# A hybrid attention layer: GpSimd's scaling of attention weights with a second multiplication by 1.0

## The chip, the cores and the metric

One core of a Trainium2 chip runs the kernel. The metric is the device time of one execution in microseconds (us), lower is better; the median over runs is compared. A core has five engines with queues of their own: TensorE (PE), VectorE (DVE), ScalarE (ACT), GpSimd (POOL) and SyncE (SP), which here only starts DMAs.

## What is computed

A decoder layer on a sequence of 256 tokens of width 1024, in float32. The input is normalised and multiplied by one wide matrix; its columns feed three token mixers and their gates. Cut to what matters here:

```python
z = rmsnorm(x, g_in) @ w_in          # queries, keys, values, gates of three mixers
ya = moba_attention(mq, mk, mv)      # 8 heads of 64; with 256 tokens: causal attention
yb = dsa_attention(dq, dk, dv, ...)  # 8 heads of 64; causal, on the 64 keys an indexer selects
yc = cross_attention(xq, mem_k, mem_v)   # 4 heads of 128 into 256 memory tokens
u = sum(sigmoid(g_b) * ((y_b * silu(gate_b)) @ w_up_b) for b in (a, b, c))
out = rmsnorm(x + u @ w_out, g_final)
```

In both self-attentions (names beginning with m and d) a head's weights are `softmax(scores)`: exponentials divided by their sum over a row.

## The kernel before

Every float32 product is made of three fast ones: each operand is split into a high part (a rounded copy, made by ScalarE) and a low part (the remainder, a subtraction on VectorE), and TensorE adds high x high, high x low and low x high. The weights are streamed in about a hundred blocks (`w0`, `w1`, ...): a DMA on SyncE's queue, the copy on ScalarE (L248), the subtraction on VectorE (L249, mostly 128x1024), and then the block's matmuls (L254 to L256, L280).

The program is a list of steps, one a block of weights. Between the matmuls of a step, and before it, the "side work" of the attentions is put by hand: tables of step numbers (`M_PAIRS` and `D_PAIRS` for the two self-attentions) say after which step a function is called. The instructions of TensorE and GpSimd run in exactly that written order; those of VectorE and ScalarE are put in order by the framework's planner, which simulates the program with estimated costs:

```python
ctx.enter_context(tc.manual_schedule(engines={mybir.EngineType.PE, mybir.EngineType.Pool}))
```

Self-attention goes by pairs of heads. `self_scores` has TensorE make a pair's scores (L470), VectorE add the mask and take the maximum (L602), and ScalarE take exponentials into a tile `pr` (L606: mpr, dpr) with their sums in `st` (mst, dst). `PARTS` are the two halves of the queries: 128 queries on 128 keys (128 columns) and 128 queries on 256 keys (256 columns). Half a step later `self_scale` has VectorE take the reciprocals (L614) and GpSimd multiply the weights in place, one instruction a part (L616). `self_transpose` has TensorE transpose the scaled weights (L625: mtp, dtp), ScalarE and VectorE evacuate them in two parts (L626, L627: mph, mpl, dph, dpl), and `self_values` multiplies them by the values (L640: mya, dya) and adds the two parts (L645, L646: myT, dyT).

GpSimd's other work near these: two copies for the indexer (L439, L440) between head 0's scaling and head 1's of the first attention, and `gate_apply` (L719: a product of a normalised gate and a mixer's output), called behind the last heads of the second. VectorE takes that product up in L720. Cross-attention scales its weights on ScalarE (L672).

Of the kernel before, what the change touches and what calls it, by code (L numbers as in the profile page):

```python
# [11 lines left out]
OP = mybir.AluOpType  # L12
# [98 lines left out]
def hybrid_layer_kernel(  # L111
# [14 lines left out]
    nc = tc.nc  # L126
# [247 lines left out]
    for nm in ORDER:  # L374
# [6 lines left out]
        elif nm[0] == "u":  # L381
            b, c = int(nm[1]), int(nm[2])
# [229 lines left out]
    def self_scale(nm, hd):  # L612
        pr, st = prs[nm, hd]
        nc.vector.reciprocal(st[:, 4:6], st[:, 2:4])  # L614
        for t, c in PARTS:
            nc.gpsimd.tensor_scalar_mul(pr[:, c], pr[:, c], st[:, 4 + t : 5 + t])  # L616

    def self_transpose(nm, hd):
        pr, _ = prs.pop((nm, hd))
# [252 lines left out]
    def attend(nm, starts, bias):  # L872
        for b, (s0, s1) in enumerate(starts):
            at(s0, self_scores, nm, b, bias)
            for e in range(2):
                at(s0 + 0.5 + 0.5 * e, self_scale, nm, 2 * b + e)
                at(s1 + e, self_transpose, nm, 2 * b + e)
                at(s1 + 1 + e, self_values, nm, 2 * b + e)
# [188 lines left out]
```

## Time and profile before

| what | us |
|---|---|
| median of 3 runs | 325.01 |
| the three runs | 324.80 to 327.15 |
| the profiled execution, its own time | 326.02 |
| its span, first to last instruction | 324.2 |
| TensorE busy | 314.7 |
| VectorE busy | 252.8 |
| ScalarE busy | 202.8 |
| GpSimd busy | 55.0 |
| L616 on GpSimd, first attention (16 instructions) | 15.9 |
| L616 on GpSimd, second attention (16 instructions) | 15.0 |

Busy times are unions over one engine's instructions in the profiled execution. Matmuls are pipelined and the profile models their ends, so a busy TensorE is not one at its peak. Times on GpSimd are rougher than the others.

### The profile page before, as it was taken

What the parts mean: (1) busy time and instruction counts of PE and PEld (TensorE: products, weight loads), DVE (VectorE), ACT (ScalarE), POOL (GpSimd) and SP (SyncE); (2) the same over time, 40 slices, a digit from 0 to 9 for tenths busy, and PEclk for the clock granted to TensorE, in tenths of its full rate; (3) what the DMA queues carried; (4) which work ended last, traced back from release to release, by engine and by line L of the source; (5) the groups of instructions that cost most, each with busy time, mean ns of one, the idle gap of its engine ahead of it and who ended that gap; (6) DMA issues with size and microseconds to landing.
All of it is one profiled execution on the core that took longest, in us unless ns stands there. A gap on an engine that the chain in (4) does not pass through costs nothing.

```text
span 324.2 us, 6395 instructions
## 1 busy us (share of the span) xinstructions
PE 314.7 (97%) x2442; PEld 299.5 (92%) x2442; DVE 252.8 (78%) x458; ACT 202.8 (63%) x357; POOL 55.0 (17%) x58
## 2 busy tenths in 40 slices
PE   8999999998999999999999999999999999999992
PEld 7799999998999989889999998999999999999882
DVE  3579999998899999987776659998567775677523
ACT  5599766687777636396567596755454546643434
POOL 0000000029305000020400473321000111014011
PEclk9999999999999999999999999999999999999998
DMA  6999887865536346474343433478766566655003
GB/s 203 373 342 312 243 265 215 282 207 147 182 127 169 100 152 232 134 257 142 139 121 130 139 116 120 141 235 284 220 182 195 184 193 198 178 157 189 2 0 129
DMA packets 18367, 59.45 MB, mean 183 GB/s; under 512 B 2208, under 2 KB 2464, under 8 KB 18336
## 3 DMA queue, kind: packets, MB, share of 16 engines
q1 hardware_dynamic: 17760, 57.73, 55.9%
q10 hardware_dynamic: 576, 1.31, 1.1%
q8 instruction: 19, 0.31, 0.4%
q14 instruction: 12, 0.10, 0.1%
HBM read 55.89 MB, written 1.05 MB: 176 GB/s over the span
## 4 chain that ended last, share of the span: by engine, by line
PE 71%; DVE 15%; issue 4%; ACT 4%; DMA 2%; POOL 1%; SPq 1%; DVEq 0%; ACTq 0%; POOLq 0%
DMA w2r<-w_in 2%; PE i_0ps L280 2%; PE i_1ps L280 2%; DVE wk L498 2%; PE mv_0ps L280 1%; PE mv_1ps L280 1%; DVE m L496 1%; PE o_0ps L255 1%; PE o_0ps L254 1%; PE o_0ps L256 1%; POOL dpr L616 1%; PE dya L640 1%; PE lg L480 1%; PE o_1ps L256 1%; PE o_1ps L255 1%
## 5 line engine op out<-in xcount | busy, mean ns | idle before, releaser
L616 POOL TENSOR_SCALAR dpr<-dpr,dst 128x128 f32<-128x128 f32 (+1 forms) x16 | 15.0, 955 | 75.5 <-DVE dst L614 75.5
L616 POOL TENSOR_SCALAR mpr<-mpr,mst 128x128 f32<-128x128 f32 (+1 forms) x16 | 15.9, 1009 | 54.7 <-DVE mst L614 54.7
L745 POOL TENSOR_TENSOR u<-u,gt 128x512 f32<-128x512 f32 x7 | 9.9, 1412 | 77.1 <-DVE gt L742 77.1
L732 ACT ACTIVATE gt<-gt,x_first 128x256 f32<-128x256 f32 x24 | 10.9, 500 | 2.7 <-DVE gt L729 2.7
L606 ACT ACTIVATE dpr<-dms,dst 128x128 f32<-128x128 f32 (+1 forms) x16 | 7.1, 446 | 3.6 <-DVE dst L602 3.6
L786 ACT ACTIVATE junk<-xn 128x512 f32<-128x512 f32 (+1 forms) x5 | 2.7, 543 | 8.6 <-DVE xn L784 8.6
L606 ACT ACTIVATE mpr<-mms,mst 128x128 f32<-128x128 f32 (+1 forms) x16 | 7.1, 444 | 1.2 <-DVE mst L602 1.2
L662 ACT ACTIVATE xpr<-xsc,xst,xs_rstd 128x256 f32<-128x256 f32 x8 | 4.4, 560 | 3.3 <-DVE xst L658 3.3
L750 ACT CAST us<-u 128x512 fp32r<-128x512 f32 x4 | 2.5, 622 | 6.1 <-POOL u L745 4.9
L645 ACT COPY dyT<-dya 64x256 f32<-64x256 f32 x8 | 2.9, 367 | 4.2 <-PE dya L640 4.1
L484 ACT ACTIVATE rl<-lg 128x384 f32<-128x384 f32 x8 | 3.9, 484 | 2.7 <-PE lg L480 1.6
L487 DVE SCALAR_TENSOR_TENSOR acc<-rl,iw,acc 128x128 f32<-128x128 f32 (+1 forms) x14 | 5.3, 425 | 0.1
L790 POOL TENSOR_TENSOR xn<-xn,gf 128x512 f32<-128x512 f32 x2 | 2.6, 1288 | 16.0 <-ACT junk L786 16.0
L480 PE MATMUL lg<-ikT,iqT 128*128 128x128 f32 (+1 forms) x32 | 5.1, 281 | 0.1
L966 PE MATMUL warm<-ones 128*128 128x128 f32 x18 | 4.2, 430 | 1.0 <-DVE eps_t L961 1.0
L602 DVE CUSTOM_DVE_ANT_0 mms<-msc,bias_c 128x128 f32<-128x128 f32 (+1 forms) x16 | 5.0, 350 | 0.0
L966 PEld LDWEIGHTS warm<-ones 128*128 128x128 f32 x18 | 3.9, 331 | 1.0 <-DVE eps_t L961 1.0
L646 DVE TENSOR_TENSOR dyT<-dyT,dya 64x256 f32<-64x256 f32 x8 | 3.3, 417 | 1.9 <-ACT dyT L645 1.7
L627 DVE TENSOR_TENSOR dpl<-dtp,dph 128x384 fp32r<-128x384 f32 x8 | 4.4, 554 | 0.4
L602 DVE CUSTOM_DVE_ANT_0 dms<-dsc,sel 128x128 f32<-128x128 f32 (+1 forms) x16 | 4.7, 351 | 0.0
L626 ACT CAST dph<-dtp 128x384 fp32r<-128x384 f32 x8 | 3.8, 479 | 1.4 <-PE dtp L625 1.3
L784 DVE TENSOR_TENSOR xn<-o_0ps,xn 128x512 f32<-128x512 f32 x2 | 1.4, 692 | 4.2 <-PE o_0ps L256 4.2
(1296 smaller groups left out, 1546.1 us busy)
## 6 DMA issues: line engine op xcount, KB each, us to landing
x_rows<-x SPq DMA_DIRECT2D x2, 512.0 KB, 8.1
eT<-memT SPq DMA_DIRECT2D x4, 256.0 KB, 4.7
xn<-x SPq DMA_DIRECT2D x2, 512.0 KB, 5.7
w0r<-w_in SPq DMA_DIRECT2D x2, 256.0 KB, 3.4
w1r<-w_in SPq DMA_DIRECT2D x2, 256.0 KB, 5.1
xT<-xT SPq DMA_DIRECT2D x2, 256.0 KB, 6.8
w2r<-w_in SPq DMA_DIRECT2D x1, 512.0 KB, 7.3
w3r<-w_in ACTq DMA_DIRECT2D x1, 512.0 KB, 7.7
```

The source lines that it names most:

```text
L255: nc.tensor.matmul(ps, ah, bl, start=False, stop=False)
L256: nc.tensor.matmul(ps, al, bh, start=False, stop=last)
L280: nc.tensor.matmul(accs[nm][t][:, :n], a[p](k, slice(t * P, (t + 1) * P)), w[q][:, half, :], start=k + i == 0, stop=k + i == nk + 1,)
L480: nc.tensor.matmul(lg[:, c : c + n], q[:, q0:q1], idx["k"][:, j, 0:n], start=j == 0, stop=j == 1)
L487: nc.vector.scalar_tensor_tensor(acc[:, c], rl[:, c], iw[:, t, g : g + 1], (bias_c if g == 0 else acc)[:, c], op0=OP.mult, op1=OP.add,)
L498: nc.vector.match_replace(out=wk[:, c], in_to_replace=m8[t], in_values=src[:, c], imm_value=TAKEN)
L602: nc.vector.tensor_tensor_reduce(out=ms[:, c], in0=sc[:, c], in1=bias()[:, c], op0=OP.add, op1=OP.min, scale=-(HD**-0.5), scalar=3e38, acc ...
L606: big["last_exp"] = nc.scalar.activation(pr[:, c], ms[:, c], AF.Exp, bias=st[:, t : t + 1], scale=-1.0, accum_out=st[:, 2 + t : 3 + t],)
L616: nc.gpsimd.tensor_scalar_mul(pr[:, c], pr[:, c], st[:, 4 + t : 5 + t])
L732: nc.scalar.activation(gt[:, f, :], gt[:, f, :], AF.Sigmoid, bias=x_first[:, j : j + 1])
L745: adder.tensor_tensor(u, u, gt, op=OP.add)
L966: nc.tensor.matmul(warm[:, 0:P], ones, ones, start=True, stop=True)
```

## The change

In `self_scale`, GpSimd's multiplication by a factor for each partition (query) is written as an instruction with two operations: by the factor, and then by the constant 1.0. Before, the second operation was empty.

```diff
         nc.vector.reciprocal(st[:, 4:6], st[:, 2:4])
         for t, c in PARTS:
-            nc.gpsimd.tensor_scalar_mul(pr[:, c], pr[:, c], st[:, 4 + t : 5 + t])
+            nc.gpsimd.tensor_scalar(
+                pr[:, c], pr[:, c], st[:, 4 + t : 5 + t], 1.0, op0=OP.mult, op1=OP.mult
+            )
```

## Rows read from the trace of the kernel before

**Rows 1.** The page: busy times by engine, and the chain's shares by engine.
```profile
PE 314.7 (97%) x2442; PEld 299.5 (92%) x2442; DVE 252.8 (78%) x458; ACT 202.8 (63%) x357; POOL 55.0 (17%) x58
...
PE 71%; DVE 15%; issue 4%; ACT 4%; DMA 2%; POOL 1%; SPq 1%; DVEq 0%; ACTq 0%; POOLq 0%
```

**Rows 2.** A window of 100 us: busy time by engine, clock, DMA share, GB/s.
```profile
200.00:300.00 100.00, 100.00 (x833) 99.18 (x832) 74.63 (x75) 55.04 (x73) 16.05 (x11) 1.00 0.63 195
```

**Rows 3.** Waits of TensorE: line <- releaser, us in total, times, longest.
```profile
PE mv_0ps L280 <- ACT w2h L248: 0.3, 1, 0.3
```

**Rows 4.** Groups by line and shape, GpSimd: busy us, mean ns, idle before.
```profile
L616 POOL TENSOR_SCALAR dpr<-dpr,dst 128x256 f32<-128x256 f32 x8 | 8.4, 1048 | 0.0
...
L616 POOL TENSOR_SCALAR dpr<-dpr,dst 128x128 f32<-128x128 f32 x8 | 6.9, 862 | 75.5 <-DVE dst L614 75.5
...
L790 POOL TENSOR_TENSOR xn<-xn,gf 128x512 f32<-128x512 f32 x2 | 2.6, 1288 | 16.0 <-ACT junk L786 16.0
...
L905 POOL COPY bias_c<-cst 128x128 f32<-128x128 f32 x1 | 0.3, 308 | 25.6 <-DMA cst<-consts 25.6
```

**Rows 5.** Single instructions of L616: ns min/median/max, first and last start us.
```profile
L616 POOL TENSOR_SCALAR dpr<-dpr,dst x1: 603/603/603, 143.5 to 143.5; 128x128 f32<-128x128 f32 x1
...
L616 POOL TENSOR_SCALAR dpr<-dpr,dst x1: 922/922/922, 144.1 to 144.1; 128x256 f32<-128x256 f32 x1
...
L616 POOL TENSOR_SCALAR dpr<-dpr,dst x1: 1925/1925/1925, 180.6 to 180.6; 128x256 f32<-128x256 f32 x1
```

**Rows 6.** All instructions of L616, first attention and sequencer.
```profile
L616 POOL TENSOR_SCALAR mpr<-mpr,mst x16: 594/918/1680, 68.4 to 100.3; 128x128 f32<-128x128 f32 x8, 128x256 f32<-128x256 f32 x8
...
L616 POOLq MODIFY_POOL_CONFIG  x2: 4/4/4, 27.0 to 27.0; - x2
```

**Rows 7.** Timelines, 73 to 78 us: start, length, instruction, [idle before it <- releaser].
```profile
73.94 4.59 POOL L616 TENSOR_SCALAR mpr<-mpr,mst 128x128 f32<-128x128 f32 x3
...
77.23 6.63 POOL L616 TENSOR_SCALAR mpr<-mpr,mst 128x128 f32<-128x128 f32 x8
...
75.26 1.20 DVE L249 TENSOR_TENSOR w29l<-w29r,w29h 128x1024 fp32r<-128x1024 f32 x1
76.39 0.54 DVE L627 TENSOR_TENSOR mpl<-mtp,mph 128x384 fp32r<-128x384 f32 x1
...
76.98 0.38 PE L640 MATMUL mya<-mpl,mv 128*128 128x256 f32 x1 [0.91 <-DVE mpl L627]
...
77.38 0.29 PE L625 MATMUL mtp<-cst,mpr 128*128 128x128 f32 x1
```

**Rows 8.** Timelines of GpSimd and TensorE, 178 to 181 us.
```profile
178.52 1.50 POOL L616 TENSOR_SCALAR dpr<-dpr,dst 128x128 f32<-128x128 f32 x2 [16.72 <-DVE dst L614]
...
180.43 0.38 PE L625 MATMUL dtp<-cst,dpr 128*128 128x128 f32 x2
```

**Rows 9.** The chain that ended last, 187 to 193 us: start, us, what.
```profile
187.94 0.77 POOL dpr L616 x2
...
189.42 2.54 POOL dpr L616 x2
191.96 1.28 POOL mgzn L719
```

**Rows 10.** Timelines of TensorE and VectorE, 189 to 198 us.
```profile
189.33 0.49 PE L625 MATMUL dtp<-cst,dpr 128*128 128x128 f32 x2
...
193.28 0.29 PE L625 MATMUL dtp<-cst,dpr 128*128 128x128 f32 x1
...
193.87 2.32 DVE L249 TENSOR_TENSOR w60l<-w60r,w60h 128x1024 fp32r<-128x1024 f32 x1
...
197.26 0.35 PE L640 MATMUL dya<-dph,dv 128*128 128x256 f32 x1 [0.67 <-DVE dyT L646]
```

**Rows 11.** Timeline of VectorE, 71 to 73 us.
```profile
71.74 0.27 DVE L602 CUSTOM_DVE_ANT_0 mms<-msc,bias_c 128x128 f32<-128x128 f32 x1
...
72.17 0.69 DVE L436 TENSOR_TENSOR iqs<-iq,iqs 128x512 fp32r<-128x512 f32 x1
```

## The prediction

> **What bounds the kernel now.** I read the page first, then the windows, then the waits of TensorE, then the line that changes, and last the few microseconds around each use of it. The page shows TensorE busy for 97% of the span and carrying 71% of the chain that ended last, with GpSimd at 17% of the span and 1% of the chain [rows 1]. From 200 to 300 us the window of TensorE has no idle time at all [rows 2], so what is lost before 200 us is carried to the end, and nothing later gives it back. In the list of what TensorE waited for, the warm-up apart, two waits are larger than 0.3 us, which is the next [rows 3]: 0.91 us before the values product of the second attention stage's first head at 76.98 us [rows 7], and 0.67 us before another at 197.26 us [rows 10]. These two are all that a quicker GpSimd could buy, 1.6 us together, and only where it is GpSimd that is late.
>
> The changed line is L616, 32 instructions: 16 heads, each with one of 128 columns and one of 256. Undisturbed, the first takes 603 ns and the second 922 ns [rows 5], so 128 more columns cost 319 ns: 2.5 ns a column over a fixed 0.28 us (603 less 319). The group means are higher, 862 and 1048 ns [rows 4], because some instructions stand still beside a wide subtraction on VectorE: the slowest, 1925 ns, begins at 180.6 us [rows 5].
>
> **The change, part by part.** It removes 32 multiplications by a column of factors with an empty second slot, and adds 32 with a multiplication by 1.0 in that slot. Tiles, sizes, engine, order on GpSimd, semaphores and DMAs stay as they are. A multiplication by 1.0 changes no value, so nothing downstream has other data.
>
> What one of the new instructions costs is not in the trace: every tensor-scalar instruction of GpSimd in it is one of L616. I bound it from both sides.
> - From above: the second slot repeats all that the first does for a column. 128 columns then cost 0.60 + 0.32 = 0.92 us and 256 cost 0.92 + 0.64 = 1.56 us, which is 0.95 us more a head.
> - From below: the nearest row without arithmetic is the copy of 128 columns, 308 ns [rows 4], half of the 603. If the two-slot form ran like a copy, and the 256 columns took half of theirs too, a head would cost 0.31 + 0.46 = 0.77 us instead of 1.5, about 0.75 us less. A loop made for exactly this pair of operations could do that; nothing in the trace excludes it.
> - In between: a tensor-tensor multiplication of 512 columns takes 1288 ns [rows 4], at most 2.5 ns a column with its fixed part in it, though it reads twice as much. So reading does not set the pace of L616; what its loop does per column does, and that can go either way with another pair of operations.
>
> I take no change of the instruction. The nearest row is L616 itself: the same operation, input, output and columns, with a slot that its loop has to pass in either form. Both ends stay in the range.
>
> [...]
>
> [...]
>
> What lies on the path: the scalings of most heads end microseconds before the transposes that read them. The close places are three. In the first attention, head 1's two scalings start at 73.94 us, held back by the queue; the next head's starts at 77.23 and TensorE's transposes of head 1 at 77.38, a slack of 0.15 us [rows 7]. In the second attention, head 4 is done at 178.52 + 1.50 = 180.02 and transposed at 180.43, a slack of 0.41 [rows 8]. Head 6 is done at 189.42, when head 7's scaling begins [rows 9], and its transposes begin at 189.33 (the last of them needs the last columns) [rows 10]: no slack. Head 7 is done at 191.96 [rows 9] and transposed at 193.28 [rows 10], a slack of 1.3.
>
> At no change of the instruction the sum is 0: 326.02 us for the profiled execution, 324.2 of it span. That execution is 1.0 us above the median of the runs shown, 325.01, so the forecast is 325.0.
>
> **Rivals.**
> 1. The two-slot form is faster, by up to 0.75 us a head. At 76.98 us this buys nothing: TensorE there waits for a remainder on VectorE that starts at 76.39, right behind a wide subtraction of 1.20 us [rows 7], and not for GpSimd. At 197.26 us it does. GpSimd's scalings of heads 6 and 7 end at 191.96 and the gating product behind them ends 1.28 us later [rows 9]; VectorE waits for it, and so starts the wide subtraction w60l at 193.87, just as GpSimd's next gating product begins, and takes 2.32 us for it instead of about 1.2 [rows 7, 10]. Earlier scalings let w60l start earlier and pass ahead of that product; then the evacuation for which TensorE waits is some 1 us earlier and the 0.67 us go. With up to 0.1 for head 6 that is some 0.7: 325.0 - 0.7 = 324.3. For it speaks that one multiplication costs as much per column as a two-input one; against it that the trace has no instruction showing a quicker arithmetic loop.
> 2. The second multiplication is paid for, at the upper bound 0.95 us a head: slower. It decides from 0.15 us in head 1 on, where TensorE's transposes then wait 0.95 - 0.15 = 0.8. Head 4 adds 0.95 - 0.41 = 0.54, head 6 0.95, and the chain into 197.26 us is 1.9 later against a TensorE that is by then 1.5 later in this stage: 0.4. Together 2.7: 325.0 + 2.7 = 327.7. At half that price, 0.48 us a head, the same places give 0.33 + 0.07 + 0.48 + 0.4 = 1.3 and 326.3. For it speaks that L616 is paced by its loop and not by its reads; against it that the slot exists already.
> 3. VectorE's and ScalarE's streams change their order. Only TensorE's and GpSimd's are written by hand; the others are made by a planner from estimated costs, as the score evacuation L602 standing between the pieces of one index evacuation shows [rows 11]. If the planner counts the new form differently, a wide subtraction of 1.2 us can change places with an evacuation that TensorE awaits, as the one before 76.98 us does [rows 7]. One such place costs or gives back about 0.9 us; since the plan's places were chosen with the old order, I count it as a loss: 325.9.
>
> That the multiplication by 1.0 is dropped when the program is built would look like the forecast and has its time.
>
> **How the numbers follow.** No change of the instruction and the order: 0.40, with 324.5 to 325.5 as its own range. Rival 1: 0.30 (324.3). Rival 2: 0.15 (326.3 to 327.7). Rival 3: 0.15 (325.9, either way by 1 to 2 us). The range reaches down to the whole gain of rival 1 with another 0.7 us of a better order, 323.6, and up to the upper bound of rival 2, 327.7. One per cent, which is about what a measurement of this kernel can tell from no change, is 3.25 us. TensorE's two waits come to 1.6 us, so a gain beyond 1% needs a new order that also shortens what counts as busy now: 0.03. A loss beyond 1% needs more than the upper bound of rival 2, which takes a doubled loop and further stalls beside VectorE, or a bad new order: 0.08. Within 1%: 0.89.
>
> **What would show each step.** In the groups of the changed kernel, L616 keeps 16 + 16 tensor-scalar instructions; undisturbed ones at 0.60 and 0.92 us say forecast, about 0.3 and 0.5 rival 1, about 0.9 and 1.6 rival 2. TensorE's idle time before 197 us tells what became of the gain: gone for rival 1, larger for rival 2, with new waits before the transposes of heads 1, 4 and 6. The sequence of VectorE around 71 and 193 us shows whether the planner moved anything. Wrong would be the whole account if the time moved by over 1% with L616 unchanged in duration and order, or if GpSimd became much quicker and TensorE gained more than its two waits.

## The result, and the profile after

The changed kernel takes 323.6 us against 325.36 for the kernel before, medians of 18 runs each: ratio 0.9945, interval 0.9932 to 0.9958, or 1.8 us less (1.4 to 2.2). That is not the forecast of no change; it is the first rival, and more than its price.

The instruction itself changed. These are single, undisturbed instructions of L616 in the changed kernel (ns min/median/max, first and last start), to be held against [rows 5]:

```profile
L616 POOL TENSOR_SCALAR dpr<-dpr,dst x1: 372/372/372, 144.4 to 144.4; 128x128 f32<-128x128 f32 x1
...
L616 POOL TENSOR_SCALAR dpr<-dpr,dst x1: 477/477/477, 144.7 to 144.7; 128x256 f32<-128x256 f32 x1
```

603 ns became 372 and 922 became 477. The fixed part is nearly as before, 372 - 105 = 267 ns against 284; the slope fell from 2.5 ns a column to (477 - 372) / 128 = 0.82. The page's busy times by engine, and the chain's shares, show where that went:

```profile
PE 313.0 (97%) x2442; PEld 297.4 (92%) x2442; DVE 252.1 (78%) x458; ACT 202.9 (63%) x357; POOL 41.9 (13%) x58
...
PE 70%; DVE 15%; DMA 5%; ACT 4%; issue 4%; SPq 0%; ACTq 0%; DVEq 0%
```

GpSimd is busy 13.1 us less than in [rows 1] and has left the chain, yet the kernel gained 1.8 us: over 11 us of the saving lay where nobody waited. The instruction sequences of VectorE and ScalarE are the same in both programs, entry by entry, and so are those of TensorE, SyncE and, but for the one operation, GpSimd.

Most of the gain has one place. The timeline of GpSimd in the changed kernel, the line numbers behind L616 being two higher now (L721 is L719 of before):

```profile
188.81 1.70 POOL L616 TENSOR_SCALAR dpr<-dpr,dst 128x128 f32<-128x128 f32 x4 [7.73 <-DVE dst L614]
192.29 1.29 POOL L721 TENSOR_TENSOR mgzn<-mgzn,myT 128x512 f32<-128x512 f32 x1 [1.78 <-ACT mgsg L720]
194.66 1.95 POOL L721 TENSOR_TENSOR mgzn<-mgzn,myT 128x512 f32<-128x512 f32 x1 [1.08 <-ACT mgsg L720]
```

And VectorE and TensorE beside it:

```profile
193.62 0.69 DVE L722 TENSOR_TENSOR mgsg<-mgsg,mgzn 128x512 f32<-128x512 f32 x1
194.23 1.22 DVE L249 TENSOR_TENSOR w60l<-w60r,w60h 128x1024 fp32r<-128x1024 f32 x1
...
193.75 0.39 PE L642 MATMUL dya<-dpl,dv 128*128 128x256 f32 x1
...
197.29 0.28 PE L642 MATMUL dya<-dph,dv 128*128 128x256 f32 x1
...
197.52 0.22 PE L642 MATMUL dya<-dph,dv 128*128 128x128 f32 x1
```

The same instructions in the kernel before, beside those in [rows 9, 10]:

```profile
193.79 1.32 POOL L719 TENSOR_TENSOR mgzn<-mgzn,myT 128x512 f32<-128x512 f32 x1 [0.56 <-ACT mgsg L718]
...
192.88 0.39 PE L640 MATMUL dya<-dpl,dv 128*128 128x256 f32 x1
...
197.87 0.22 PE L640 MATMUL dya<-dph,dv 128*128 128x128 f32 x1
```

Before, the second gating product on GpSimd began at 193.79 and w60l on VectorE at 193.87 [rows 10], 0.08 us behind it: the product ran its 1.32 us and w60l took 2.32. Now w60l begins 0.43 us ahead of the product, takes 1.22, and it is the product that stands (1.95 us against 1.32), on which TensorE does not wait. Between TensorE's products shown, 192.88 to 197.87 before and 193.75 to 197.52 after, 4.99 us became 3.77: 1.2 us at this place, of which only 0.67 had been idle time in the profile [rows 10]. The other 0.55 us the profile draws as busy matmuls. Seen from TensorE's product (192.88 and 193.75), w60l ends 1.6 us sooner than before: it starts 0.5 us sooner and is 1.1 us shorter. The earlier start alone would not have given the 1.2.

A smaller piece lies in the first attention. There w31l (VectorE) started behind a scaling of head 5 that had 0.8 us left, and took 1424 ns; with the scaling over sooner, it takes 1224. The two instructions before, and then w31l after (ns min/median/max):

```profile
L616 POOL TENSOR_SCALAR mpr<-mpr,mst x1: 914/914/914, 83.0 to 83.0; 128x256 f32<-128x256 f32 x1
...
L249 DVE TENSOR_TENSOR w31l<-w31r,w31h x1: 1424/1424/1424, 83.1 to 83.1; 128x1024 fp32r<-128x1024 f32 x1
```
```profile
L249 DVE TENSOR_TENSOR w31l<-w31r,w31h x1: 1224/1224/1224, 84.2 to 84.2; 128x1024 fp32r<-128x1024 f32 x1
```

TensorE gains the same 0.2 us at the index transposes behind it: from the first `iqt` to the first `ikt` 0.93 us pass before and 0.71 after. 1.2 + 0.2 = 1.4 us is at the lower end of the measured interval. Whether the other 0.4 of the 1.8 is more than noise, no trace shows.

### The profile page after: what moved, and what is told of

The parts are those of the page before. It is cut to its first block, busy times and chain, and to the rows that moved or that the text cites. A ratio compares the mean times of both kernels' runs of the same rounds, so it can differ in the third digit from the quotient of the medians.

```text
span 323.0 us, 6395 instructions
## 1 busy us (share of the span) xinstructions
PE 313.0 (97%) x2442; PEld 297.4 (92%) x2442; DVE 252.1 (78%) x458; ACT 202.9 (63%) x357; POOL 41.9 (13%) x58
## 4 chain that ended last, share of the span: by engine, by line
PE 70%; DVE 15%; DMA 5%; ACT 4%; issue 4%; SPq 0%; ACTq 0%; DVEq 0%
DMA w3r<-w_in 3%; DVE wk L498 2%; DMA w25r<-w_in 2%; DVE m L496 1%; PE o_0ps L255 1%; PE o_0ps L256 1%; PE o_0ps L254 1%; DMA w0r<-w_in 1%; PE dya L642 1%; PE i_0ps L280 1%; PE i_1ps L280 1%; PE mv_1ps L280 1%; PE mv_0ps L280 1%; DVE acc L487 1%; PE lg L480 1%
## 5 line engine op out<-in xcount | busy, mean ns | idle before, releaser
L616 POOL TENSOR_SCALAR dpr<-dpr,dst 128x128 f32<-128x128 f32 (+1 forms) x16 | 6.6, 425 | 84.1 <-DVE dst L614 83.9
L616 POOL TENSOR_SCALAR mpr<-mpr,mst 128x128 f32<-128x128 f32 (+1 forms) x16 | 9.8, 629 | 56.3 <-DVE mst L614 56.3
L628 ACT CAST dph<-dtp 128x384 fp32r<-128x384 f32 x8 | 3.8, 479 | 1.4 <-PE dtp L627 1.3
L498 DVE MATCH_REPLACE8 wk<-m,wk 128x128 f32<-128x128 f32 (+1 forms) x14 | 4.7, 342 | 0.0
```

Of the source, the lines that this page charges most:

```text
L498: nc.vector.match_replace(out=wk[:, c], in_to_replace=m8[t], in_values=src[:, c], imm_value=TAKEN)
L616: nc.gpsimd.tensor_scalar(pr[:, c], pr[:, c], st[:, 4 + t : 5 + t], 1.0, op0=OP.mult, op1=OP.mult)
```

## Experiments

Ratios are to the kernel before, on the same chip. Theory A: the gain is made at the one place before 197 us. Its rival, theory B: it is spread, because GpSimd is less in VectorE's way throughout.

**Only the last two heads.**
```diff
+            if nm == "d" and hd >= 6:
+                nc.gpsimd.tensor_scalar(..., 1.0, op0=OP.mult, op1=OP.mult)
+            else:
                 nc.gpsimd.tensor_scalar_mul(pr[:, c], pr[:, c], st[:, 4 + t : 5 + t])
```


> Two-slot form for heads 6 and 7 of the second attention only, the other 28 scalings as before. Theory A (the gain is made at one place: these scalings end sooner, so the gating products behind them and the wide subtraction w60l no longer meet, and TensorE's wait of 0.67 us at 197 us goes): the whole gain of the change, 1.2 to 2.0 us, ratio 0.994 to 0.996. Theory B (the gain is spread: GpSimd is less in VectorE's way in both attentions): 4 of 32 instructions, about an eighth, 0.2 us, ratio 0.999. Side question, TensorE's pace behind 200 us (117.8 ns from matmul to matmul before, 116.7 after): if the wait at 197 us sets it, 116.7 here; if it is chance from run to run, either.

Measured: 0.9958 (0.9941 to 0.9975), 1.4 us from 4 of the 32 instructions. In the timeline of VectorE, w60l has its short time:

```profile
192.82 1.22 DVE L249 TENSOR_TENSOR w60l<-w60r,w60h 128x1024 fp32r<-128x1024 f32 x1
```

**All but the last two heads.** The same condition with `not`.

> Two-slot form for all scalings but those of heads 6 and 7 of the second attention. Theory A: nearly nothing, 0 to 0.3 us (the 0.2 us that TensorE gains at 85 us), ratio 0.999 to 1.000, with TensorE's wait near 197 us still there. Theory B: seven eighths of the gain, 1.5 us, ratio 0.995. Pace behind 200 us: 117.8 ns if the wait sets it.

Measured: 1.0006 (0.9987 to 1.0026). 28 of the 32 quicker instructions buy nothing that can be measured (the 0.2 us of w31l among them), w60l meets the product as before (timeline of VectorE), and TensorE's wait is back (its waits, us in total, times, longest):

```profile
193.78 2.32 DVE L249 TENSOR_TENSOR w60l<-w60r,w60h 128x1024 fp32r<-128x1024 f32 x1
```
```profile
PE dya L645 <- DVE dyT L651: 0.7, 1, 0.7
```

The two together settle A against B.

**The kernel before again.** No edit.

> The kernel before, once more, for the noise and for a second profile. Both theories: ratio 1.000 within 0.002, L616 at 0.60 and 0.92 us undisturbed, TensorE waiting 0.5 to 0.8 us near 197 us. Pace behind 200 us: 117.8 ns again if the wait sets it, 116.7 or 117.8 if it is chance.

Measured: 1.001 (0.9995 to 1.0026), with TensorE's wait of 0.65 us at 197.73. The side question is answered too. Windows of 90 us (busy us and count by engine), the profile of before that stands above first, then this one:

```profile
200.00:290.00 90.00, 90.00 (x767) 90.00 (x766) 66.83 (x66) 50.11 (x66) 12.62 (x9) 1.00 0.64 199
```
```profile
200.00:290.00 90.00, 90.00 (x774) 90.00 (x773) 67.98 (x67) 50.64 (x68) 13.08 (x9) 1.00 0.64 200
```

The same program, the same granted clock, the same wait ahead of it, and 767 matmuls against 774: the slower pace belongs to that one execution (the eleven other profiles of this study have the quicker pace), and the 0.9 us that it costs behind 200 us is no part of the change.

**Prices of pairs of operations.**
```diff
+        pairs = {("d", 0): (None, 0.0, OP.mult, OP.add), ("d", 1): (None, 0.0, OP.mult, OP.subtract),
+                 ("d", 2): (None, 0.0, OP.mult, OP.max), ("d", 3): (0.0, None, OP.add, OP.mult),
+                 ("d", 5): (None, ones[:, 0:1], OP.mult, OP.mult), ("d", 6): (1.0, None, OP.mult, OP.mult),
+                 ("d", 7): (0.0, None, OP.max, OP.mult), ("m", 4): (None, 3e38, OP.mult, OP.min)}
...
```


> Prices of pairs of operations, one pair a head, otherwise the changed kernel. Second attention: head 0 factor then add 0.0, head 1 factor then subtract 0.0, head 2 factor then maximum with 0.0, head 3 add 0.0 then factor, head 4 factor alone (as before), head 5 factor then a second column of ones, head 6 multiply by 1.0 then factor, head 7 maximum with 0.0 then factor; first attention: head 4 factor then minimum with 3e38, the others factor then 1.0. Weights are at least 0, so no value changes. Theory P (a loop of its own for a few pairs): multiply-multiply in either order at 0.37 and 0.48 us, and pairs with maximum, minimum or subtract at 0.9 and more for the 256 columns, as the empty slot. Theory Q (every filled pair runs on the short loop, only the empty slot is slow): all filled pairs at 0.37 and 0.48 us, only head 4 of the second attention at 0.60 and 0.92. The pointer to a second column costs its own read on top in both.

Single undisturbed instructions of this run: factor then minimum (first two rows), factor then add (two), factor then subtract (its 256 columns), factor then maximum (its 256 columns), 1.0 then factor (two), and the empty slot (L628):

```profile
L632 POOL TENSOR_SCALAR mpr<-mpr,mst x1: 725/725/725, 81.4 to 81.4; 128x128 f32<-128x128 f32 x1
...
L632 POOL TENSOR_SCALAR mpr<-mpr,mst x1: 1145/1145/1145, 82.1 to 82.1; 128x256 f32<-128x256 f32 x1
...
L632 POOL TENSOR_SCALAR dpr<-dpr,dst x1: 379/379/379, 144.2 to 144.2; 128x128 f32<-128x128 f32 x1
...
L632 POOL TENSOR_SCALAR dpr<-dpr,dst x1: 489/489/489, 144.5 to 144.5; 128x256 f32<-128x256 f32 x1
...
L632 POOL TENSOR_SCALAR dpr<-dpr,dst x1: 1155/1155/1155, 145.7 to 145.7; 128x256 f32<-128x256 f32 x1
...
L632 POOL TENSOR_SCALAR dpr<-dpr,dst x1: 1144/1144/1144, 159.2 to 159.2; 128x256 f32<-128x256 f32 x1
...
L632 POOL TENSOR_SCALAR dpr<-dpr,dst x1: 376/376/376, 188.6 to 188.6; 128x128 f32<-128x128 f32 x1
...
L632 POOL TENSOR_SCALAR dpr<-dpr,dst x1: 482/482/482, 189.0 to 189.0; 128x256 f32<-128x256 f32 x1
...
L628 POOL TENSOR_SCALAR dpr<-dpr,dst x1: 607/607/607, 179.2 to 179.2; 128x128 f32<-128x128 f32 x1
...
L628 POOL TENSOR_SCALAR dpr<-dpr,dst x1: 923/923/923, 179.8 to 179.8; 128x256 f32<-128x256 f32 x1
```

The prices are those of theory P, with one more quick pair than expected: multiply-multiply in either order and multiply-add run at 0.8 to 0.9 ns a column; a pair with minimum at (1145 - 725) / 128 = 3.3, dearer than the empty slot's 2.5, one with subtract at the same 3.3 (733 ns for its 128 columns), and 256 columns of factor then maximum take 1144 ns. A second column in place of the constant costs a little more, 443 ns for 128 columns against 372. The loops of theory P are in no trace; the prices are all that the run shows. The prediction's "either way" was the right question: with another operation in the second slot the same edit would have made the instruction dearer, as the second rival has it.

The run's trace also shows that a little is enough, though head 7's scaling is a slow pair here. (Its single time, 324.57 us, lies within the spread of both kernels and tells nothing.) Its timelines of GpSimd, VectorE and TensorE:

```profile
192.29 1.29 POOL L735 TENSOR_TENSOR mgzn<-mgzn,myT 128x512 f32<-128x512 f32 x1
194.44 2.15 POOL L735 TENSOR_TENSOR mgzn<-mgzn,myT 128x512 f32<-128x512 f32 x1 [0.87 <-ACT mgsg L734]
...
194.22 1.22 DVE L249 TENSOR_TENSOR w60l<-w60r,w60h 128x1024 fp32r<-128x1024 f32 x1
...
193.53 0.39 PE L656 MATMUL dya<-dpl,dv 128*128 128x256 f32 x1
```

TensorE's product of 192.88 in the kernel before stands at 193.53 here, so this execution is 0.65 us behind at that point; the first gating product, at 192.29 - 0.65 = 191.64, is then about 0.3 us earlier than in [rows 9], and w60l already starts 0.22 us ahead of the second product. TensorE's last product shown above, 197.87 in the kernel before, stands at 197.32 here: 3.79 us behind 193.53, the gain of the changed kernel at this place.

**The gating product late again, the weights early.**
```diff
+        if (nm, hd) == ("d", 7):
+            for t, c in PARTS:
+                nc.gpsimd.tensor_scalar_mul(scratch[:, c], bias_c[:, c], st[:, 4 + t : 5 + t])
```


> The changed kernel, and behind the scalings of the second attention's head 7 two more multiplications with an empty slot by GpSimd, of 128 and 256 columns, into a tile that nobody reads (extra work, no value changes). The weights are as early as in the changed kernel; the gating products behind them on GpSimd are as late as before. Theory A1 (the gating product is what the gain hangs on: VectorE's product behind it and then w60l start late and meet the second gating product): the 1.2 us are lost again, TensorE's wait near 197 us is back and w60l takes about 2.3 us, ratio 0.999 to 1.000. Theory A2 (the weights' own arrival at TensorE matters): the gain stays, ratio 0.994 to 0.996, w60l 1.2 us.

Measured: 0.9995 (0.9977 to 1.0014): the gain is gone though TensorE's weights are as early as in the changed kernel. GpSimd's products and w60l are where they were before, 0.21 us apart and in the bad order (timelines of GpSimd and VectorE):

```profile
193.56 1.44 POOL L725 TENSOR_TENSOR mgzn<-mgzn,myT 128x512 f32<-128x512 f32 x1 [0.44 <-ACT mgsg L724]
...
193.77 2.32 DVE L250 TENSOR_TENSOR w60l<-w60r,w60h 128x1024 fp32r<-128x1024 f32 x1
```

TensorE's wait is back with them (its waits, us in total, times, longest):
```profile
PE dya L646 <- DVE dyT L652: 0.8, 1, 0.8
```

So it is theory A1: the scaling's own reader does not matter here, the instruction queued behind it on GpSimd does.

**A slow pair everywhere.**
```diff
-                pr[:, c], pr[:, c], st[:, 4 + t : 5 + t], 1.0, op0=OP.mult, op1=OP.mult
+                pr[:, c], pr[:, c], st[:, 4 + t : 5 + t], 0.0, op0=OP.mult, op1=OP.max
```


> The same edit with the maximum with 0.0 in the second slot instead of the multiplication by 1.0 (weights are at least 0, so no value changes). By the prices measured, 0.73 and 1.15 us, 0.35 us more a head than the empty slot. By the slacks of the prediction: head 1 of the first attention 0.2 us, head 4 of the second none (slack 0.41), head 6 0.35. Theory A with a race at 197 us (the wide subtraction has already lost to the gating product, and a later start costs nothing more): 0.4 to 0.6 us slower than before, ratio 1.001 to 1.002. Rival (every delay of GpSimd's chain goes on into 197 us, as the prediction had it): 0.7 to 1.0 us, ratio 1.002 to 1.003. If TensorE does not wait for the scalings at all: 1.000.

Measured: 1.0005 (0.999 to 1.0019). The interval excludes the rival, just, but cannot tell theory A from no change. TensorE's waits show both the price and what hides it:

```profile
PE dya L642 <- DVE dyT L648: 1.0, 1, 1.0
PE mya L642 <- DVE mpl L629: 0.9, 1, 0.9
...
PE dtp L627 <- POOL dpr L616: 0.2, 1, 0.2
```

Head 6's transposes now do wait for GpSimd, and the wait at 197 us is 0.35 us longer; but w31l now starts in the last 0.27 us of a scaling and loses nothing (1.23 us; the scaling behind it stands instead, 1563 ns), which gives 0.2 us back, and the products at 193 us, which had waited in the kernel before, come 0.3 us sooner against their neighbours. Theory A's "a later start costs nothing more" does not hold at 197 us: w60l keeps its 2.31 us, and its later start goes on into the wait. The time cannot tell 0.2 us from nothing, so of the second rival's places only those that show in this profile are confirmed: head 6 with 0.2 us of idle time for 0.35 and 197 us with 0.35 for 0.4; not head 1, whose transposes moved by less than 0.1 us.

**The wait at 77 us, by moving TensorE's work.**
```diff
-M_PAIRS = ((23, 25.5), ...
+M_PAIRS = ((23, 26), ...
```


> The changed kernel with the first attention's first pair transposed and multiplied half a step later (25.5 to 26 in the table of steps), so that TensorE has other matmuls while VectorE's remainder is queued behind two wide subtractions at 77 us. If that wait of 0.97 us goes and no new one comes: 0.6 to 1.0 us less than the changed kernel, ratio to before 0.991 to 0.993. If the two pairs' transposes then crowd in the one bank that they share: 0.994 to 0.997.

Measured: 1.0004 (0.9989 to 1.0019), 1.9 us more than the changed kernel. The wait went and a larger one came, for a scaling on GpSimd (TensorE's waits):

```profile
PE mtp L627 <- POOL mpr L616: 1.3, 1, 1.3
...
PE mya L642 <- DVE myT L648: 0.6, 1, 0.6
PE iqt L453 <- DVE mst L602: 0.4, 1, 0.4
```

A variant that moves only the values products and the second head's transposes:
```diff
+                late = 0.5 if (nm, b) == ("m", 0) else 0
-                at(s1 + e, self_transpose, nm, 2 * b + e)
-                at(s1 + 1 + e, self_values, nm, 2 * b + e)
+                at(s1 + e + late * e, self_transpose, nm, 2 * b + e)
+                at(s1 + 1 + e + late, self_values, nm, 2 * b + e)
```


> As the one before, but only the first pair's values products and the second head's transposes go half a step later, the first head's transposes stay. Same expectation: 0.991 to 0.993 if the wait of 0.97 us at 77 us goes without a new one, 0.994 to 0.997 if another takes its place.

Measured: 1.0006 (0.9992 to 1.002), with the same three new waits. Both missed the gain that was expected.

**The wait at 77 us, by VectorE's order.**
```diff
...
+                if s == 29:
+                    order.enter_context(tc.issue_after(big["first_pl"]))
                 nc.vector.tensor_sub(lo[:, ks, :], raw[:, ks, :], hi[:, ks, :].bitcast(F32))
...
```


> The changed kernel with one pair of VectorE's instructions changed over by an ordering edge: the remainder mpl of the first attention's first head goes ahead of the wide subtraction w29l. TensorE waits 0.97 us for that remainder at 78.05 us in the changed kernel; without w29l in front it is due about 1 us earlier, and head 1's scalings behind it are not stopped by w29l either. If TensorE's wait there is real time: 0.7 to 1.0 us less than the changed kernel, ratio to before 0.991 to 0.993. If another wait takes its place (head 1's transposes for GpSimd's scaling, or w29l late for its matmuls): 0.994 to 0.996.

Measured: 0.9945 (0.9926 to 0.9964), no different from the changed kernel. The wait of 0.97 us is gone and others came for it, 0.4 us for the index transposes (`iqt`) and 0.2 for `ikt`, until TensorE was where it had been. The window shows why (columns PE, PEld, DVE, ACT, POOL busy):

```profile
64.00:78.00 14.00, 13.96 (x120) 12.90 (x119) 13.83 (x48) 11.37 (x29) 6.81 (x12) 1.00 0.56 172
```

VectorE is busy 13.83 of 14 us there, so the changed order only decided which of TensorE's instructions waited for it.

**The kernel before, with w60l ahead.**
```diff
...
+            if (b, hf) == (0, 0):
+                order.enter_context(tc.issue_after(big["w60l"]))
             nc.vector.tensor_tensor(sg, sg, zn, op=OP.mult)
...
```


> The kernel before, with its slow scalings, and one ordering edge on VectorE: the wide subtraction w60l goes ahead of the product mgsg that waits for GpSimd, so w60l can begin when its own input is there and does not meet the second gating product at its start. Some later products of the gates on VectorE and ScalarE fall one place back with it. Theory A (the collision of w60l with the gating product is the loss, whatever makes it): w60l takes 1.2 us, TensorE's wait near 197 us goes, and the kernel is as fast as the changed one there without any quicker scaling: 1.0 to 1.4 us, ratio 0.995 to 0.997. Rival (GpSimd's time itself is the loss): 0.999 to 1.001.

Measured: 0.9988 (0.997 to 1.0006), the rival's range and not theory A's. w60l takes 1.22 us as theory A has it, but the collision passed on to VectorE's next instruction, a product that started 0.57 us behind GpSimd's and paid instead (timelines of GpSimd and VectorE):

```profile
194.02 1.79 POOL L723 TENSOR_TENSOR mgzn<-mgzn,myT 128x512 f32<-128x512 f32 x1 [0.58 <-ACT mgsg L722]
...
193.45 1.22 DVE L249 TENSOR_TENSOR w60l<-w60r,w60h 128x1024 fp32r<-128x1024 f32 x1 [0.39 <-ACT w60h L248]
194.59 1.78 DVE L727 TENSOR_TENSOR mgsg<-mgsg,mgzn 128x512 f32<-128x512 f32 x1
```

VectorE's product takes 0.69 us alone, as in the changed kernel at 193.62. TensorE waits 0.6 us behind it for `dpl`, a neighbour of the old place. So the run did not take the collision away, and its time cannot decide between the two. The trace of the run on pairs does: there the first gating product was only 0.3 us earlier than in the kernel before, w60l was 1.1 us shorter, and TensorE had the whole 1.2 us. A version that beats the changed kernel was not found.

## Why the prediction was wrong

- **What bounds the kernel:** held in part. TensorE carries what is lost before 200 us to the end (it is busy for all of the 90 us behind it, in both windows above), and GpSimd's time as such is not the bound: 13.1 us less of it gave 1.8. What did not hold is the ceiling, "These two are all that a quicker GpSimd could buy, 1.6 us together": of the two places only one was GpSimd's, and it gave 1.2 us for 0.67 of idle time. Whether the whole gain passes 1.6, the sign of being wrong that the prediction named, 1.8 (1.4 to 2.2) leaves open.
- **The price of the instruction:** this is the step that failed: "I take no change of the instruction. The nearest row is L616 itself", with "a slot that its loop has to pass in either form". The filled slot made the instruction quicker. A head costs 372 + 477 = 849 ns instead of 603 + 922 = 1525, or 0.68 us less, close to the 0.75 of the bound from below. The row that spoke for it was read and not followed: one input at 2.5 ns a column, where an instruction with two inputs took no more with its fixed part included [rows 4]. That the slot has to be passed in either form was the author's assumption; no run shows the loops, only what the pairs cost.
- **Rival 1:** right in the mechanism, place and order of events, and right that 76.98 us gives nothing (that place is `mya`, in the first attention and not in the second, as the prediction's first paragraph has it). Its size was too small: 0.67 us for the place at 197 us was the idle time alone, and 1.2 came back, since 0.5 us of waiting stood inside matmuls that count as busy. The 0.2 us of w31l were not seen at all. It was given 0.30, less than the forecast's 0.40.
- **Rival 2:** not what happened, but a dearer second operation exists: a maximum costs 0.35 us more a head (726 ns for 128 columns with it in the first slot, 1144 for 256 with it in the second, against 603 and 922), less than the 0.48 of its cheaper case. At all heads it came to no measurable loss, since waits elsewhere shrank; the sums of 1.3 and 2.7 us for 0.48 and 0.95 were not tried.
- **Rival 3:** fell. The planner left every sequence as it was.
- **The range:** its lower end, 323.6, is the measured median, but by luck: it was rival 1 with another 0.7 us from a better order of VectorE and ScalarE, and no order changed. Within 1% was given 0.89 and is what happened.

## What to carry to other kernels

Price an instruction of GpSimd by its pair of operations, not by its name: here multiply-multiply and multiply-add cost 0.8 to 0.9 ns a column and an empty second slot 2.5, so a neutral second operation made it quicker. Read what stands behind an instruction on its own queue as well as who reads its result: nearly all of the gain hung on a product queued behind the scalings, and whether it began just before or after a wide subtraction on VectorE. Where GpSimd and VectorE held each other up here, the order of two starts was worth 1.1 us (the subtraction took 2.32 us when 0.08 us behind the product, and 1.22 when 0.22 or 0.43 ahead), so look for pairs that start close together at the places where TensorE waits.

## What the runs showed of the hardware

- The second slot filled with a multiplication by 1.0 made GpSimd's tensor-scalar quicker: 372 and 477 ns against 603 and 922 for 128 and 256 columns. Minimum and subtract in it made it slower, 725 and 1145 for minimum, 733 and 1155 for subtract, and so did maximum, 1144 for 256 columns.
- Of GpSimd's second gating product and the subtraction w60l on VectorE, the one that began first took 1.32 us (the product, in the kernel before) or 1.22 (w60l, in the changed one), and the other paid nearly all that was left of it: w60l 2.32 us when 0.08 us behind, the product 1.95 when 0.43 behind. In the run with the gating product late again, w60l 0.21 us behind, the product took 1.44 and w60l 2.32. Behind a scaling it was less: w31l started with 0.8 us of the scaling left and took 0.2 longer.
- TensorE ran the same matmuls behind 200 us about 1% slower in one execution than in another at the same granted clock of 1.00, 767 against 774 in 90 us. What sets it was not found.
